# The output gate's panels of a gated linear attention, spread between its heads

## The chip, the cores and the metric

The kernel runs on one core of a Trainium2 chip. The metric is the device time of one execution in microseconds (us), as the median of several runs. TensorE is called PE, VectorE DVE, ScalarE ACT, SyncE SP, GpSimd POOL, as in the profile.

## The reference, cut to what matters

A decoder trunk of two layers over 256 tokens of width 2048, in fp32: a layer with gated linear attention (GLA), a layer with forgetting attention, cross-attention into 256 memory tokens in both, and a gated feed-forward network behind each. The change lies in the GLA layer alone, whose mixer is:

```python
def gla_mixer(h, mem_k, mem_v, w_in, w_gate_up, b_gate, gn_gain, w_out):
    z = h @ w_in
    q, k, v, glr, og, mq = split_cols(z, [...])
    g = jax.nn.log_sigmoid((glr @ w_gate_up + b_gate).astype(jnp.float32)) / GLA_GATE_TAU
    o = gla_chunked(split_heads(q, 4) * (256 ** -0.5), split_heads(k, 4), split_heads(v, 4), split_heads(g, 4))
    o = o * lax.rsqrt(jnp.mean(o * o, axis=-1, keepdims=True) + EPS)
    o = o * gn_gain.astype(jnp.float32).reshape(4, 1, 384)
    o = merge_heads(o).astype(h.dtype) * jax.nn.silu(og)
    m = memory_attention(mq, mem_k, mem_v)
    return jnp.concatenate([o, m], axis=-1) @ w_out
```

There are 4 heads with keys of 256 and values of 384. The output gate `og` has 1536 columns; it meets the heads' normed output only in the product with `silu(og)`.

## The kernel before

Every projection goes through weight panels. A panel's weights come from HBM in units of 512 KB (384 KB for values) on SP's queue (L198); each unit is split by ACT into a rounded part `whi` (a cast, L201) and by DVE into the residual `wlo` (L210). There are 4 buffers for raw units, 3 for `whi` and 4 for `wlo`. `proj_fm` multiplies a panel of 256 columns: 4 units, for each of two 128-column halves 16 matmuls with `whi` over 512 columns (L239) and 16 with `wlo` over 256 (L237). Its result has the features on the partitions; `whole` adds its two halves (ACT L246, DVE L248). `proj_tm` multiplies a panel of values or of the output projection, in 8 units (L276); a unit is 12 matmuls.

The GLA function takes the heads one after the other; they are called head 0 to head 3 here. For each head stand, in the program's order: the gates (`gates`: a matmul L585, then Abs, Exp and Ln on ACT at L588 to L590, and on DVE L592 to L594, which gives `bc`), the panels for q and k, the panel for v (head 0's v was made ahead), and the core (`core`). The core builds decays with Exp on ACT (L603, L604, L610, L626, L633) and products on DVE, runs small matmuls (L646 to L668), copies their results through masks into `att` (DVE L677, L690), multiplies by v (L697, L698, through the single buffer `ps_o`, which ACT empties at L701), and norms the result (L339, a Newton iteration of small DVE instructions, `dg` at L373, the matmuls L375, the row L378 and the scaling L706) into `on`, three 128-wide slices for each head.

`take_og(j)` multiplies panel j of the output gate, which covers the slices 2j and 2j+1, and makes the mix: DVE L713, Silu on ACT (L714), the product with `on` (DVE L715), and a split into two parts (ACT L311, DVE L312). Slices 0 to 2 need head 0, 3 to 5 head 1, 6 to 8 head 2, 9 to 11 head 3. The gate's tile takes one of five buffers with the tag `tmp`, which the gates of the heads use too. Before, panels 0 and 1 stand behind head 3's k and ahead of its v, and panels 2 to 5 behind head 3's core. The output projection follows; it takes the memory heads' slices 12 to 15 first, then 0 to 11 in order.

A planner sets the order of instructions on each engine from the program's order, priorities (weight units are drawn ahead by 300 instructions) and its own estimates. A core's first matmuls are held until the last projection panel of values has ended (`issue_after(ends[-1].ins)`). Each engine then works strictly in its order. Where the functions of ACT change between table sets, the builder puts in loads of the table.

Of the kernel before, what the change touches and what calls it, by code (L numbers as in the profile page):

```python
# [25 lines left out]
GLA_H, DK, DV = 4, 256, 384  # L26
# [11 lines left out]
NUNIT = 1024  # L38
AHEAD = 300

OG_EARLY = 2
WARM = 12

FV_PARTS = ((0, 376), (376, 764), (764, 1152), (1152, 1536))
# [10 lines left out]
def _panels():  # L55

    full = list(range(KC))
    out = []  # L60

    def fm(key, w, c0, kcs=full, second=None):
        cols = [(c0, 256)] if second is None else [(c0, 128), (second, 128)]
        out.append((key, w, kcs, cols, 4))

    def tm(key, w, c0, n, kcs=full, more=()):
        out.append((key, w, kcs, [(c0, n), *more], 2))

    for l in range(2):
        for j in range(2):  # L70
            fm(("mk", l, j), ("mem_w_kv", l), j * 256)
        tm(("mv", l), ("mem_w_kv", l), 512, 512)
    tm(("gv", 0), ("gla_w_in", 0), G_V, DV, more=[(G_R, RANK)])
    for j in range(2):
        fm(("mq", 0, j), ("gla_w_in", 0), G_MQ + j * 256)
    for h in range(GLA_H):
        fm(("gq", h), ("gla_w_in", 0), G_Q + h * DK)
        fm(("gk", h), ("gla_w_in", 0), G_K + h * DK)
        for j in range(OG_EARLY if h == GLA_H - 1 else 0):
            fm(("og", j), ("gla_w_in", 0), G_OG + j * 256)  # L80
        if h:
            tm(("gv", h), ("gla_w_in", 0), G_V + h * DV, DV)
    for j in range(OG_EARLY, 6):
        fm(("og", j), ("gla_w_in", 0), G_OG + j * 256)
    late = list(range(12, 16)) + list(range(12))

    def ffn(l):
        for p, (lo, hi) in enumerate(PARTS):
            for j in range(lo, hi):
                fm(("up", l, j), ("ffn_w_up", l), j * P, second=HID + j * P)  # L90
            for f in range(4):
                tm(("down", l, p, f), ("ffn_w_down", l), f * 512, 512, list(range(lo, hi)))

    for f in range(4):
        tm(("wo", 0, f), ("gla_w_out", 0), f * 512, 512, late)
    ffn(0)
    for j in range(6):
        fm(("fk", j), ("fox_w_kv", None), F_K + j * 256)
    for j, (lo, hi) in enumerate(FV_PARTS):
        more = [] if j else [(F_L, FOX_H)]  # L100
        tm(("fv", j), ("fox_w_kv", None), F_V + lo, hi - lo, more=more)
    for j in range(2):
        fm(("mq", 1, j), ("fox_w_in", 0), FOX_H * HD + j * 256)
    for j in range(6):
        fm(("fq", j), ("fox_w_in", 0), j * 256)
    for f in range(4):
        tm(("wo", 1, f), ("fox_w_out", 0), f * 512, 512, late)
    ffn(1)
    return out
# [29 lines left out]
def _trunk(ctx: ExitStack, tc: tile.TileContext, xt, xtok, memt, wp, wgu, gns, gfin, cnv, par, msk, out):  # L139
# [73 lines left out]
    def proj_fm(key, src, evac, before=None):  # L213

        units = where[key]
        acc = [pacc.tile([P, 512], F32, name="acc", tag="acc") for _ in range(2)]
        base = min(min(u[1]) for u in units)
        if before is None:  # L220
            turns = [(0, 0), (1, 0), (0, 1), (1, 1), (2, 1), (3, 1), (2, 0), (3, 0)]
        else:
            turns = [(0, 0), (0, 1), (1, 0), (1, 1), (2, 0), (2, 1), (3, 1), (3, 0)]
        ready = {}
        for u, low in turns:
            if u not in ready:
                if before is None:
                    ready[u] = split_unit(units[u])
                else:
                    ready[u] = split_unit(units[u], 2, lambda half: before(u, half), whole=u > 0)  # L230
            w = ready[u][low]
            for j, kc in enumerate(units[u][1]):
                both = src[kc - base]
                for c in range(2):
                    s = slice(j * 256 + c * P, j * 256 + (c + 1) * P)
                    if low:
                        TE.matmul(acc[c][:, :T], w[:, s], both[:, 0, :], start=False, stop=False)  # L237
                    else:
                        TE.matmul(acc[c], w[:, s], both, start=u == j == 0, stop=(u, j) == (3, 3))  # L239
        for c in range(2):  # L240
            evac(c, acc[c])

    def whole(a):

        t = sm.tile([P, T], F32, name="part1", tag="part1")
        S.activation(t, a[:, T:], AF.Copy)  # L246
        r = sm.tile([P, T], F32, name="wholes", tag="wholes")
        V.tensor_tensor(r, a[:, :T], t, ALU.add)  # L248
        return r
# [57 lines left out]
    def split(dst, i, src, g=None):  # L307

        hi, lo = dst[i][:, 0, :], dst[i][:, 1, :]
        if g is None:  # L310
            S.activation(hi, src, AF.Copy)  # L311
            V.tensor_tensor(lo, src, hi.bitcast(F32), ALU.subtract)  # L312
        else:
            S.activation(hi, src, AF.Copy, scale=g)
            V.scalar_tensor_tensor(lo, src, g, hi.bitcast(F32), ALU.mult, ALU.subtract)  # L315
# [93 lines left out]
    def place(buf, i, name, dtype=F32R):  # L409

        return const.tile([P, 2, T], dtype, name=f"{name}{i}", tag=f"{buf}{i}")
# [119 lines left out]
    def gla(nx):  # L531
        h, mix = bufB, bufA
        with tc.tile_pool(name="gla", bufs=1) as gp:
# [9 lines left out]
            def values(hd):  # L543
                return gp.tile([P, 2, DV], F32, name="gv", tag="gv", bufs=2)
# [29 lines left out]
            def gates(hd):  # L574

                bc = gp.tile([P, 2, T], F32, name="bc", tag="bc", bufs=2)
                raw = gp.tile([P, DK], F32, name="wgraw", tag="wgraw")
                nc.sync.dma_start(raw, wgu[hd])
                wg = gp.tile([P, DK], F32R, name="wg", tag="wg")
                S.activation(wg, raw, AF.Copy)  # L580
                V.tensor_tensor(wg[32:64], raw[32:64], wg[32:64].bitcast(F32), ALU.subtract)
                for c in range(2):
                    f = 2 * hd + c
                    ps = work("s", 2)
                    TE.matmul(ps[:, :T], wg[:, c * P : (c + 1) * P], glr, start=True, stop=True)  # L585
                    bias = part[:, C_BG + f : C_BG + f + 1]
                    e = gp.tile([P, T], F32, name="ge", tag="tmp", bufs=5)
                    S.activation(e, ps[:, :T], AF.Abs, bias=bias)  # L588
                    S.activation(e, e, AF.Exp, scale=-1.0)
                    S.activation(e, e, AF.Ln, bias=1.0)  # L590
                    mz = gp.tile([P, T], F32, name="gm", tag="tmp", bufs=5)
                    V.tensor_scalar(mz, ps[:, :T], bias, 0.0, ALU.add, ALU.min)  # L592
                    V.tensor_tensor(mz, mz, e, ALU.subtract)
                    V.tensor_tensor_scan(bc[:, c, :], scanmask, mz, 0.0, ALU.mult, ALU.add)  # L594
                return bc
# [112 lines left out]
            def take_og(j):  # L708
                def evac(c, a):
                    i = 2 * j + c  # L710
                    mix[i] = place("A", i, "mix")
                    g = gp.tile([P, T], F32, name="gate", tag="tmp", bufs=5)
                    V.tensor_tensor(g, whole(a), nx.row(), ALU.mult)  # L713
                    S.activation(g, g, AF.Silu)  # L714
                    V.tensor_tensor(g, g, on[i], ALU.mult)  # L715
                    split(mix, i, g)

                proj_fm(("og", j), h, evac)

            for hd in range(GLA_H):  # L720
                bc = gates(hd)
                q = gp.tile([P, 2, T], F32, name="gq", tag="gq", bufs=2)
                k = gp.tile([P, 2, T], F32, name="gk", tag="gk", bufs=2)
                v = values(hd) if hd else v0
                proj_fm(("gq", hd), h, lambda c, a: V.scalar_tensor_tensor(
                    q[:, c, :], whole(a), DK ** -0.5, nx.row(), ALU.mult, ALU.mult))
                proj_fm(("gk", hd), h, lambda c, a: V.tensor_tensor(k[:, c, :], whole(a), nx.row(), ALU.mult))
                if hd == GLA_H - 1:
                    for j in range(OG_EARLY):
                        take_og(j)  # L730
                if hd:
                    proj_tm(("gv", hd), h, lambda b, a: S.activation(
                        v[:, b, :], a, AF.Copy, scale=nx.col()[:, b : b + 1]))
                core(hd, q, k, v, bc)
            for j in range(OG_EARLY, 6):
                take_og(j)


# [146 lines left out]
    def preparing(name, dst, also=None):  # L885
# [18 lines left out]
        return n, then  # L904

    gla(nx)
    n, then = preparing("ffn0", bufB)
    add_out(("wo", 0), bufA, then)
# [132 lines left out]
```

## Time and profile before

| | us |
|---|---|
| median of 3 runs (2284.77 to 2284.79) | 2284.78 |
| the profiled execution | 2284.61 |
| its span | 2282.8 |
| PE busy | 2270.1 (99%) |
| DVE busy | 1602.8 (70%) |
| ACT busy | 1249.9 (55%) |

The heads of the GLA layer run between about 160 and 330 us of the span, the output projection from 379 us on. In a row of a timeline or of groups, `x` is the number of instructions, and `<-` names what released a wait.

### The profile page before, as it was taken

How to read it: one execution, taken by the hardware profiler on the slowest of the kernel's cores; microseconds unless marked ns; L12 is line 12 of the kernel's file. 1: busy time of each engine (PE TensorE's matmuls, PEld its weight loads, DVE VectorE, ACT ScalarE, POOL GpSimd, SP SyncE). 2: the span in 40 equal slices, each digit the busy share in tenths (PEclk: the TensorE clock that was granted, in tenths of full speed). 3: DMA queues.
4: the chain of work that ended last, by engine and by line, in shares of the span. 5: the costliest groups of instructions: out<-in, count | busy, mean ns of one | idle time of the engine just before them, and what ended most of it. 6: DMA issues, size and time to landing. Idle time of an engine off the chain costs nothing.

```text
span 2282.8 us, 33321 instructions
## 1 busy us (share of the span) xinstructions
PE 2270.1 (99%) x12420; PEld 1984.6 (87%) x12420; DVE 1602.8 (70%) x2691; ACT 1249.9 (55%) x1981; POOL 3.4 (0%) x19
## 2 busy tenths in 40 slices
PE   9999999999999999999999999999999999999998
PEld 8989988888888888888888998888888888888886
DVE  8579987577765777557766567657776577756775
ACT  7565555555643555445565556556554455534554
POOL 0000000000000000000000000000000000000000
PEclk9999999999999999999999999999999999999999
DMA  9655556555666565666655665555656556665664
GB/s 327 197 165 160 161 160 192 187 184 185 185 200 193 186 195 185 194 191 188 194 185 184 180 198 160 174 190 184 193 186 194 187 192 191 192 194 186 190 193 155
DMA packets 125034, 430.16 MB, mean 188 GB/s; under 512 B 14140, under 2 KB 19144, under 8 KB 124744
## 3 DMA queue, kind: packets, MB, share of 16 engines
q1 hardware_dynamic: 124440, 427.24, 59.3%
q8 instruction: 97, 1.59, 0.3%
q10 hardware_dynamic: 432, 0.79, 0.1%
q14 instruction: 65, 0.53, 0.1%
HBM read 425.87 MB, written 2.11 MB: 187 GB/s over the span
## 4 chain that ended last, share of the span: by engine, by line
PE 98%; DVE 2%; issue 0%; DMA 0%; ACT 0%; DVEq 0%
PE acc L239 38%; PE acc L276 36%; PE acc L237 20%; DVE wlo L210 1%; PE ps_s L898 0%; PE ps_t L407 0%; PE ps_s L653 0%; PE ps_o L428 0%; PE ps_s L428 0%; DVE A L315 0%; PE ps_s L810 0%; PE ps_o L826 0%; DVE att L690 0%; PE ps_o L697 0%; DMA raw<-wp 0%
## 5 line engine op out<-in xcount | busy, mean ns | idle before, releaser
L210 DVE TENSOR_TENSOR wlo<-raw,whi 128x1024 fp32r<-128x1024 f32 (+4 forms) x812 | 970.9, 1197 | 581.2 <-ACT whi L201 578.4
L201 ACT ACTIVATE whi<-raw 128x1024 fp32r<-128x1024 f32 (+4 forms) x812 | 841.1, 1037 | 746.0 <-PE acc L276 341.1
L239 PE MATMUL acc<-B,whi 128*128 128x512 f32 x2112 | 503.4, 391 | 0.0
L239 PEld LDWEIGHTS acc<-B,whi 128*128 128x128 f32 x2112 | 389.0, 188 | 75.9
L276 PE MATMUL acc<-whi,mix 128*128 128x512 f32 x1280 | 320.2, 390 | 0.0
L239 PE MATMUL acc<-mix,whi 128*128 128x512 f32 x1248 | 307.7, 391 | 0.0
L276 PEld LDWEIGHTS acc<-whi,mix 128*128 128x128 f32 x1280 | 239.7, 188 | 49.8
L237 PEld LDWEIGHTS acc<-B,wlo 128*128 128x128 f32 x2112 | 267.8, 191 | 9.5 <-DVE wlo L210 1.8
L237 PE MATMUL acc<-B,wlo 128*128 128x256 f32 x2112 | 273.3, 283 | 1.4 <-DVE wlo L210 1.4
L239 PEld LDWEIGHTS acc<-mix,whi 128*128 128x128 f32 x1248 | 228.9, 188 | 44.1
L276 PE MATMUL acc<-whi,B 128*128 128x512 f32 (+3 forms) x960 | 217.6, 362 | 0.0
L276 PEld LDWEIGHTS acc<-whi,B 128*128 128x128 f32 x960 | 174.7, 188 | 17.9
L276 PE MATMUL acc<-wlo,mix 128*128 128x512 f32 x640 | 174.8, 390 | 0.0
L237 PE MATMUL acc<-mix,wlo 128*128 128x256 f32 x1248 | 163.1, 284 | 0.0
L237 PEld LDWEIGHTS acc<-mix,wlo 128*128 128x128 f32 x1248 | 158.3, 191 | 4.5
L276 PEld LDWEIGHTS acc<-wlo,mix 128*128 128x128 f32 x640 | 119.8, 188 | 24.5
L239 PE MATMUL acc<-A,whi 128*128 128x512 f32 x544 | 134.7, 391 | 0.0
L246 ACT ACTIVATE part<-acc 128x256 f32<-128x256 f32 x240 | 90.9, 379 | 61.6 <-PE acc L239 61.2
L276 PE MATMUL acc<-wlo,B 128*128 128x512 f32 (+3 forms) x480 | 121.4, 363 | 0.0
L239 PEld LDWEIGHTS acc<-A,whi 128*128 128x128 f32 x544 | 101.8, 189 | 21.1 <-DVE A L315 0.2
L872 ACT ACTIVATE cv<-u,cw 128x256 f32<-128x256 f32 x176 | 105.0, 598 | 24.6 <-DVE u L868 24.6
L248 DVE TENSOR_TENSOR wholes<-acc,part 128x256 f32<-128x256 f32 x240 | 100.2, 418 | 0.5 <-ACT part L246 0.2
(224 smaller groups left out, 1605.8 us busy)
## 6 DMA issues: line engine op xcount, KB each, us to landing
raw<-wp SPq DMA_DIRECT2D x743, 512.0 KB, 3.7
raw<-wp SPq DMA_DIRECT2D x32, 384.0 KB, 3.5
raw<-wp SPq DMA_DIRECT2D x24, 388.0 KB, 3.5
raw<-wp SPq DMA_DIRECT2D x8, 400.0 KB, 3.1
xf<-xt SPq DMA_DIRECT2D x16, 128.0 KB, 4.5
x<-xtok SPq DMA_DIRECT2D x4, 512.0 KB, 6.4
mt<-memt SPq DMA_DIRECT2D x3, 512.0 KB, 6.3
cb<-cdram SPq DMA_DIRECT2D x12, 128.0 KB, 3.1
```

The lines of the kernel that those rows point to most:

```text
L201: casts.append(S.activation(hi[:, s], raw[:, s], AF.Copy))
L210: V.tensor_tensor(lo[:, s], raw[:, s], hi[:, s].bitcast(F32), ALU.subtract)
L237: TE.matmul(acc[c][:, :T], w[:, s], both[:, 0, :], start=False, stop=False)
L239: TE.matmul(acc[c], w[:, s], both, start=u == j == 0, stop=(u, j) == (3, 3))
L246: S.activation(t, a[:, T:], AF.Copy)
L248: V.tensor_tensor(r, a[:, :T], t, ALU.add)
L276: mm = TE.matmul(acc[b][:, :n], src[kc - base][:, part, xs], w, start=u == 0 and low == part == j == 0, stop=u == end and low == 1 and j = ...
L872: S.activation(r, u[:, 2:], AF.Identity, bias=w[3], scale=w[2])
```

## The change

One panel of the output gate moves ahead of head 1's values, one ahead of head 2's, two (panels 2 and 3) stand ahead of head 3's, and panels 4 and 5 behind its core. The list of panels in HBM and the program's order change together. Nothing is computed differently.

```diff
-OG_EARLY = 2
+OG_AT = {1: (0,), 2: (1,), 3: (2, 3)}
...
         fm(("gk", h), ("gla_w_in", 0), G_K + h * DK)
-        for j in range(OG_EARLY if h == GLA_H - 1 else 0):
+        for j in OG_AT.get(h, ()):
             fm(("og", j), ("gla_w_in", 0), G_OG + j * 256)
         if h:
             tm(("gv", h), ("gla_w_in", 0), G_V + h * DV, DV)
-    for j in range(OG_EARLY, 6):
+    for j in range(4, 6):
         fm(("og", j), ("gla_w_in", 0), G_OG + j * 256)
...
                 proj_fm(("gk", hd), h, lambda c, a: V.tensor_tensor(k[:, c, :], whole(a), nx.row(), ALU.mult))
-                if hd == GLA_H - 1:
-                    for j in range(OG_EARLY):
-                        take_og(j)
+                for j in OG_AT.get(hd, ()):
+                    take_og(j)
                 if hd:
                     proj_tm(("gv", hd), h, lambda b, a: S.activation(
                         v[:, b, :], a, AF.Copy, scale=nx.col()[:, b : b + 1]))
                 core(hd, q, k, v, bc)
-            for j in range(OG_EARLY, 6):
+            for j in range(4, 6):
                 take_og(j)
```

## The prediction

> **What bounds the kernel now.** I read the page's busy shares first, then TensorE's waits, then a table of windows over the gated-linear-attention (GLA) part, then the timelines around the two waits.
>
> ```profile
> span 2282.8 us, 33321 instructions
> ...
> PE 2270.1 (99%) x12420; PEld 1984.6 (87%) x12420; DVE 1602.8 (70%) x2691; ACT 1249.9 (55%) x1981; POOL 3.4 (0%) x19
> ```
>
> ```profile
> PE acc L237 <- DVE wlo L210: 1.6, 2, 1.4
> PE ps_o L697 <- DVE att L690: 1.1, 1, 1.1
> ```
>
> TensorE (PE) works 2270.1 of 2282.8 us, so moving panels can save only idle time; the waits above are each us in all, times, longest. Two places carry them (start, length, instructions, idle before in brackets):
>
> ```profile
> 279.02 0.67 PE L697 MATMUL ps_o<-att,gv 128*128 128x256 f32 x2 [1.11 <-DVE att L690]
> ...
> 294.19 1.22 PE L237 MATMUL acc<-B,wlo 128*128 128x256 f32 x8 [1.38 <-DVE wlo L210]
> ...
> 313.57 1.55 PE L276 MATMUL acc<-whi,B 128*128 128x384 f32 x8
> ...
> 315.65 1.55 PE L276 MATMUL acc<-whi,B 128*128 128x384 f32 x8
> ...
> 345.16 0.60 PE L697 MATMUL ps_o<-att,gv 128*128 128x256 f32 x2
> ...
> 360.33 4.00 PE L237 MATMUL acc<-B,wlo 128*128 128x256 f32 x32
> 364.16 5.64 PE L239 MATMUL acc<-B,whi 128*128 128x512 f32 x24
> 369.64 0.28 PE L375 MATMUL ps_t<-dg,onesr 128*128 128x256 f32 x1
> ```
>
> Both come from VectorE (DVE), 1.11 + 1.38 = 2.49 us, while head 3's q, k and the first output-gate (og) panels run. The last rows give PE's rates: 32 matmuls of 256 columns in 3.83 us (0.12 each), 24 of 512 in 5.48 (0.228), a 384-wide unit of 12 in 2.08. An og panel (32 + 32 matmuls) is therefore 11.1 us of PE, wherever it stands. Why DVE is late is in the windows (us, then PE, weight loads, DVE and ACT busy): the whole head stretch, the tail behind it, and the three windows from one head's mask copies (L677) to the next head's.
>
> ```profile
> 160.00:320.00 160.00, 157.45 (x1084) 144.23 (x1083) 151.74 (x375) 97.57 (x176) 0.00 (x0) 1.00 0.50 155
> 320.00:380.00 60.00, 60.00 (x404) 54.16 (x404) 43.52 (x95) 31.46 (x53) 0.00 (x0) 1.00 0.59 180
> 194.57:231.72 37.15, 37.15 (x273) 34.78 (x272) 35.55 (x85) 23.19 (x41) 0.00 (x0) 1.00 0.56 176
> 231.72:270.68 38.96, 38.96 (x287) 36.69 (x287) 37.76 (x102) 22.78 (x42) 0.00 (x0) 1.00 0.50 157
> 270.68:332.51 61.83, 59.28 (x395) 54.08 (x395) 54.93 (x136) 36.95 (x65) 0.00 (x0) 1.00 0.53 166
> ```
>
> DVE is busy 151.7 of 160 us among the heads, 43.5 of 60 behind them, with ACT at 97.6 and the granted clock 1.00. PE bounds the kernel; DVE is all but level with it here. All numbers are for this profiled execution: 2284.61 us, 1.8 over its span; the three runs' median is 2284.78, 0.17 more, which I add at the end. A measurement of this kernel can tell about 0.2%, 4.6 us, from no change.
>
> **The change part by part.** I compared the changed kernel's order of instructions on each engine with this one's. PE's is the same up to head 1's values and again from early in the output projection's second panel; matmuls are as many as before. Weight loads move with their panels on SyncE's queue; nothing is added there, and where the loads of the gate weights (L578) now stand, the buffers they wait for come free before those of the weight units behind them: nothing.
>
> *Moved DVE work.* An og panel brings DVE four residual casts (L210), and for two slices each an addition, two products and a residual (L248, L713, L715, L312).
>
> ```profile
> L210 DVE TENSOR_TENSOR wlo<-raw,whi 128x1024 fp32r<-128x1024 f32 x63 | 76.6, 1220 | 20.3 <-ACT whi L201 19.8
> L210 DVE TENSOR_TENSOR wlo<-raw,whi 128x768 fp32r<-128x768 f32 x24 | 22.8, 953 | 2.9 <-ACT whi L201 2.7
> L248 DVE TENSOR_TENSOR wholes<-acc,part 128x256 f32<-128x256 f32 x29 | 12.1, 419 | 0.4 <-ACT part L246 0.2
> ```
>
> With 0.42 for each 256-wide piece that is 4 x 1.22 + 8 x 0.42 = 8.2 us beside PE's 11.1: each panel gives DVE up to 2.9 us of air. Head 3's window had two panels and keeps two. The window from head 1's mask copies to head 2's gains PE 11.1 us (38.96 to 50.1) and DVE more than one panel's work, since og 0's products with head 0's normed output fall into it too: 5 casts, 4 additions and 9 pieces of gates, 5 x 1.22 + 13 x 0.42 = 11.6 (37.76 to 49.3). It stays level: no air where it was wanted.
>
> *Added table loads.* The diff does not show this. Silu (L714) belongs to another set of ACT's tables than the heads' Exp and Ln. Before, all Silus come behind the last head's Exps, and one load serves (first row). In the changed order ACT's queue goes Exp, Silu, Ln, Silu, Exp among heads 1 to 3, and once Silu has been in, the builder loads separately for Exp and for Ln: I count 21 loads in place of 7, 15 in place of one in GLA. An Exp–Ln pair of that kind runs later in this kernel (second fence):
>
> ```profile
> 305.05 1.28 ACT L714 ACT_TABLE_LOAD   x1
> 308.50 0.82 ACT L714 ACTIVATE gate<-gate 128x256 f32<-128x256 f32 x2 [2.16 <-DVE gate L713]
> ```
>
> ```profile
> 1291.69 0.48 ACT L760 ACTIVATE fe<-ps_s,part 128x256 f32<-128x256 f32 x1 [0.32 <-PE ps_s L302]
> 1292.18 1.28 ACT L761 ACT_TABLE_LOAD   x1
> 1293.48 0.42 ACT L761 ACTIVATE fe<-fe 128x256 f32<-128x256 f32 x1
> 1293.80 0.84 ACT L201 ACTIVATE whi<-raw 128x776 fp32r<-128x776 f32 x1
> ```
>
> Abs ends at 1292.17, Exp begins at 1293.48: 1.30 us, or 1.4 for independent neighbours, which otherwise overlap by 0.1 (Exp's 0.42 from 1293.48 reaches past the cast's start at 1293.80). Fourteen are 18.2 us more for ACT, on 97.6 in 160: it has the room in sum, but it works in order, and behind a load stand the casts (L201) that PE and DVE want and the evacuations (L701) that free the single ps_o. [...]
>
> ACT's pieces:
>
> ```profile
> L201 ACT ACTIVATE whi<-raw 128x1024 fp32r<-128x1024 f32 x63 | 66.6, 1058 | 44.2 <-PE acc L239 18.4 <-PE acc L276 7.1 <-issue 5.4
> L201 ACT ACTIVATE whi<-raw 128x768 fp32r<-128x768 f32 x24 | 20.3, 846 | 21.2 <-PE acc L239 12.3 <-PE acc L276 7.0 <-DVE att L690 1.2
> ...
> L714 ACT ACTIVATE gate<-gate 128x256 f32<-128x256 f32 x12 | 4.9, 413 | 2.2 <-DVE gate L713 2.2
> L701 ACT ACTIVATE onorm<-ps_o 128x256 f32<-128x256 f32 x12 | 4.6, 380 | 6.5 <-PE ps_o L698 6.5
> ```
>
> Now each window, from the end of a head's last L668:
>
> - *A, head 0's core beside og 0 and head 1's values.* PE runs 24 x 0.228 + 32 x 0.12 + 0.24 + 2 x 0.6 + 5 x 2.08 = 21.2 us to the sixth unit of values. ACT starts on head 0's first output (L701) when PE has done 21 x 0.228, 32 x 0.12, one L585 and the first pair of L697 and L698 (0.6): 9.4, with the hand-over 9.5. Up to that unit's cast lie 4 casts (0.85), a 384-wide Exp and 14 smaller pieces (0.4), 9.5 us less 0.1 each for overlap = 7.6, and 4 loads at 1.4 = 5.6: ready at 22.7. PE waits 1.5; the bounds are 0 (ACT has the casts done ahead of the loads) and 5.6 (all four show). I take 1.5, the sum. DVE, which waits on the same queue, comes into the next window some 1.5 late.
> - *B, head 1's core beside head 2's q and k and og 1.* DVE is level with PE (49.3 to 50.1), comes 1.5 late and waits for one load (1.3) in the middle of its gate chain. og 1's casts stand in the first half, before the window's 0.8 of margin has come: late by 1.5 + 1.3 = 2.8, which I take; at least 1.5 - 0.8 = 0.7 (the load hides), at most 1.5 + 3 x 1.3 = 5.4 (three loads stand in that chain).
> - *C, head 2's core beside head 3's q and k.* 4 loads stand between the first gate matmul (L585, behind 16 x 0.228 + 27 x 0.12 = 6.9) and the evacuation that frees ps_o for the head's third L697, due at 19.5 (head 3's q, 11.1; two pairs of L697 and L698 and two L585, 1.4; in k another 16 and 27, 6.9). ACT: 4 casts at 1.06, 11 pieces at 0.4, less 1.4 overlap = 7.2, plus 5.6, from 7.3: 20.1, with the hand-overs about 20.5. PE waits 1.0 (0 to 3). Behind that two og panels and values give DVE 4 us and more: no other wait.
> - *Tail: two panels behind head 3 in place of four.* PE reaches the output projection 22.2 us earlier, but head 3's norm does not come earlier:
>
> ```profile
> 365.55 0.76 DVE L373 TENSOR_TENSOR dg<-mask,y 128x256 fp32r<-128x256 f32 x2
> ...
> 372.56 1.27 DVE L706 SCALAR_TENSOR_TENSOR onorm<-onorm,part,row 128x256 f32<-128x256 f32 x3
> ```
>
> The dg stands 33 us behind the mask copies of 332.51. The projection starts 24 behind them (two panels, 22.2, and three pairs of L697 and L698) and goes through 6 units (12 x 0.228 = 2.7) before it needs slice 8, at 40.4, and slice 9 after 12 matmuls more (2.7), at 43.1: the order puts the next panel's first 8 there. L375 stands in the sixth unit (38.6), so row and three onorms are done at 41 and slice 9 at 42. Cover 1 us; expected cost 0, up to 3 if the row slips.
>
> Sum: -2.49 + 1.5 + 2.8 + 1.0 + 0 = +2.8: 2284.61 + 2.8 + 0.17 = **2287.6 us**, +0.12%, within what counts as no change; by the upper bounds 5.6 + 5.4 + 3 + 3 - 2.5 = +14.5, by the lower -2.49 + 0.7 = -1.8. [...]
>
> **The rivals.**
> 1. *Slower: DVE pays for the loads.* Eight loads stand between a piece that DVE hands to ACT and the one it waits for back (gate halves and the first Exp on bc, heads 1 to 3). DVE has 8.3 us idle in 160, so if ACT is never ahead, all land on PE: 8 x 1.3 = 10.4 for 2.49, +7.9: 2284.61 + 7.9 + 0.17 = 2292.7. For: DVE's queue is in order and full. Against: the loads run ahead of their operands (305.05, while Silu came at 308.50 when DVE delivered), so part hides. It decides from over 7.1 us of PE waits in A to C. 0.27.
> 2. *The loads hide and the old waits go*: each panel's 2.9 us of air covers both, 2284.61 - 2.49 + 0.17 = 2282.3. For: ACT is idle 62 of 160 us. Against: window B gets no air. 0.15.
> [...]
> 4. *Faster by over 0.2%*: PE would need 4.6 us; it idles 2.49 here. 0.01.
>
> **How the numbers follow.** Forecast (2284.0 to 2289.4) 0.54, rivals 0.27, 0.15, 0.03, 0.01. Within 0.2%: 0.54 + 0.15 = 0.69; slower 0.27 + 0.03 = 0.30; faster 0.01. The range takes in rival 2 and most of rival 1: 2282.0 to 2292.5.
>
> **What would show it.** 15 table loads of 1.28 in GLA; no wait of 1.11 and 1.38 as above, but waits of PE on a values cast (L276 <- L201) beside head 1's values, on L210 in og 1, on L701 beside head 3's k; none in the tail. Wrong if PE idles over 7 us among the heads, if the loads show gaps behind them, or if the output projection waits for mix.

## The result, and the profile after

The changed kernel takes 2288.64 us (median of 22 runs, 2287.23 to 2289.83); the kernel before, 2284.78 (22 runs, 2284.55 to 2285.03). That is +3.86 us, a ratio of 1.0016 with a 95% interval of 1.0010 to 1.0022: within what was counted as no change, on the slow side. The profiled execution took 2288.87 us, with a span of 2287.1.

Busy time of the engines, then TensorE's waits over the whole span (us in all, times, longest):

```profile
PE 2273.3 (99%) x12420; PEld 1986.0 (87%) x12420; DVE 1604.8 (70%) x2691; ACT 1266.4 (55%) x1995; POOL 3.4 (0%) x19
```

```profile
PE acc L237 <- DVE wlo L210: 2.9, 3, 1.8
...
PE ps_o L697 <- ACT onorm L701: 0.5, 1, 0.5
PE acc L276 <- ACT whi L201: 0.3, 1, 0.3
```

ACT does 16.5 us more with 14 instructions more: the table loads, of 1.28 us each. The two old waits are gone (no L697 waits for att any more), and others stand in their place. PE's busy time grew by 3.2 us although it executes the same 12420 matmuls: some of them run slower. The timeline of PE shows where (idle before in brackets):

```profile
217.17 1.68 PE L276 MATMUL acc<-whi,B 128*128 128x384 f32 x8 [0.32 <-ACT whi L201]
...
258.39 1.22 PE L237 MATMUL acc<-B,wlo 128*128 128x256 f32 x8 [0.62 <-DVE wlo L210]
261.44 1.47 PE L237 MATMUL acc<-B,wlo 128*128 128x256 f32 x8 [1.83 <-DVE wlo L210]
262.71 2.76 PE L276 MATMUL acc<-whi,B 128*128 128x384 f32 x8
...
310.52 0.70 PE L697 MATMUL ps_o<-att,gv 128*128 128x256 f32 x2 [0.45 <-ACT onorm L701]
...
383.46 1.99 PE L276 MATMUL acc<-whi,A 128*128 128x512 f32 x8
```

The eight matmuls at 262.71 take 2.76 us; eight of that shape took 1.55 in the kernel before. The windows around them (us; PE, weight loads, DVE, ACT busy; the third number from the end is the granted clock):

```profile
258.79:262.20 3.41, 1.58 (x13) 1.38 (x13) 3.41 (x10) 3.10 (x4) 0.00 (x0) 1.00 0.37 115
262.20:265.61 3.41, 3.41 (x14) 3.41 (x14) 3.32 (x7) 0.53 (x2) 0.00 (x0) 0.50 0.49 137
```

In 3.41 us PE worked 1.58; for the 3.41 us behind that its clock was granted at half. The last row of the timeline is the output projection's first: 383.46, against 379.23 before. All of the loss therefore arises ahead of it (0.36 of these 4.23 us already at the start of the kernel, where two short waits fell differently), and behind it neither kernel's PE waits.

### The profile page after: what moved, and what is told of

Same layout as the page of the kernel before. It is cut to its first block, busy times and chain, and to the rows that moved or that the text cites. A ratio compares the mean times of both kernels' runs of the same rounds, so it can differ in the third digit from the quotient of the medians.

```text
span 2287.1 us, 33330 instructions
## 1 busy us (share of the span) xinstructions
PE 2273.3 (99%) x12420; PEld 1986.0 (87%) x12420; DVE 1604.8 (70%) x2691; ACT 1266.4 (55%) x1995; POOL 3.4 (0%) x19
## 4 chain that ended last, share of the span: by engine, by line
PE 97%; ACT 1%; DVE 1%; issue 0%; DMA 0%; SPq 0%; DVEq 0%
PE acc L239 38%; PE acc L276 36%; PE acc L237 20%; PE ps_s L897 0%; PE ps_s L653 0%; DVE wlo L210 0%; PE ps_t L407 0%; ACT whi L201 0%; PE ps_o L428 0%; PE ps_s L428 0%; DMA mt<-memt 0%; PE ps_s L809 0%; PE ps_o L825 0%; PE ps_o L697 0%; PE ps_s L808 0%
## 5 line engine op out<-in xcount | busy, mean ns | idle before, releaser
L210 DVE TENSOR_TENSOR wlo<-raw,whi 128x1024 fp32r<-128x1024 f32 (+4 forms) x812 | 970.9, 1197 | 576.6 <-ACT whi L201 574.2
```

The costliest lines, as they stand in the source:

```text
L210: V.tensor_tensor(lo[:, s], raw[:, s], hi[:, s].bitcast(F32), ALU.subtract)
```

## The experiments

Theory 1 was the prediction's: the table loads hold up ScalarE's queue, and the new waits come from that. Theory 2: the places of the panels cost by themselves, and the loads hide. "Before" is the kernel before, run beside each; its median was 2284.66 to 2284.75.

**The loads taken out, all else kept.** PE's and DVE's orders of instructions are the changed kernel's, one for one.

```
-                    S.activation(g, g, AF.Silu)
+                    S.activation(g, g, AF.Silu if j > 3 else AF.Copy)
```

> The changed kernel with Silu left out of og panels 0 to 3 (Copy in its place, so their gates are not the reference's; panels 4 and 5 keep it): TensorE's and VectorE's orders are those of the changed kernel instruction for instruction, and only the 14 extra table loads are gone. Theory 1 (the loads make ScalarE late, and TensorE's waits in heads 1 to 3 and the half-clock stretch behind them come from that): those waits go and with them the 3.4 us at half clock, so the time falls to 2282.0 to 2283.5, below the kernel before, since the two old waits of 1.11 and 1.38 us are not there either. Theory 2 (where the panels stand is what costs: VectorE is level with TensorE beside head 2's q and k, and the loads hide in ScalarE's idle time): the time stays at 2287 to 2289.

Measured: 2286.29 us (11 runs, 2284.95 to 2287.5), ratio to before 1.0007 (0.9998 to 1.0016). Neither theory: 2.35 us below the changed kernel, yet 1.6 above the kernel before. The three windows from one head's last L668 to the next one's, first of the changed kernel, then of this one, say where the loads cost:

```profile
194.55:233.37 38.82, 38.50 (x283) 35.70 (x279) 35.09 (x83) 27.74 (x47) 0.00 (x0) 1.00 0.50 159
233.37:290.21 56.84, 54.27 (x358) 49.43 (x354) 51.84 (x134) 37.56 (x62) 0.00 (x0) 0.97 0.52 162
290.21:358.49 68.28, 67.83 (x452) 62.10 (x448) 57.86 (x131) 46.37 (x73) 0.00 (x0) 1.00 0.53 167
```

```profile
194.21:232.04 37.83, 37.83 (x283) 35.79 (x279) 36.01 (x90) 23.03 (x43) 0.00 (x0) 1.00 0.53 172
232.04:288.32 56.28, 53.99 (x358) 49.49 (x355) 50.72 (x128) 30.95 (x57) 0.00 (x0) 0.97 0.49 159
288.32:355.87 67.55, 67.55 (x453) 62.02 (x449) 58.32 (x131) 38.95 (x67) 0.00 (x0) 1.00 0.52 168
```

The loads cost 0.99 in the first, 0.56 in the second and 0.73 in the third, 2.28 together, close to the 2.35 between the medians. In the middle window PE idles 2.3 us without any load, and the clock is 0.97 there as well. PE and, at the same place, VectorE:

```profile
256.51 1.22 PE L237 MATMUL acc<-B,wlo 128*128 128x256 f32 x8 [0.46 <-DVE wlo L210]
259.57 1.73 PE L237 MATMUL acc<-B,wlo 128*128 128x256 f32 x8 [1.84 <-DVE wlo L210]
261.10 2.62 PE L276 MATMUL acc<-whi,B 128*128 128x384 f32 x8
```

```profile
253.70 1.62 DVE L625 TENSOR_TENSOR gdd<-bc 128x256 f32<-128x256 f32 x5
255.24 1.22 DVE L210 TENSOR_TENSOR wlo<-raw,whi 128x1024 fp32r<-128x1024 f32 x1
256.38 1.21 DVE L625 TENSOR_TENSOR gdd<-bc 128x384 f32<-128x384 f32 x3
257.48 0.56 DVE L605 TENSOR_TENSOR gq<-gq,ge 128x384 f32<-128x384 f32 x1
257.95 0.43 DVE L248 TENSOR_TENSOR wholes<-acc,part 128x256 f32<-128x256 f32 x1
258.29 1.23 DVE L210 TENSOR_TENSOR wlo<-raw,whi 128x1024 fp32r<-128x1024 f32 x1
```

No row of VectorE has an idle time: it works without a break, and between the cast that ends the first wait (255.24) and the one that ends the second (258.29) stand five pieces of head 2's gates and k. This wait is VectorE's queue, not ScalarE's loads.

**The loads alone.** Orders of PE and DVE are the kernel before's; behind one Silu on a gate weight the builder loads separately for Exp and for Ln, 12 more loads.

```
-                S.activation(wg, raw, AF.Copy)
+                S.activation(wg, raw, AF.Silu if hd == 2 else AF.Copy)
```

> The kernel before with one Copy of a gate weight (for head 2) replaced by Silu, so that gate is not the reference's; from there on Exp and Ln load a table each, as in the changed kernel: 12 more loads among heads 1 to 3, and TensorE's and VectorE's orders are untouched. Theory 1 (loads): the two old waits stay and the loads' waits come on top; without the air of a moved panel at least the changed kernel's time, 2288 to 2293. Theory 2 (placement): loads alone cost nothing, 2284.5 to 2285.5.

Measured: 2289.98 us (9 runs, 2289.37 to 2291.17), ratio 1.0024 (1.0015 to 1.0034): +5.3. As theory 1 had it. PE's waits in the heads:

```profile
PE acc L237 <- DVE wlo L210: 3.2, 3, 1.4
PE ps_o L697 <- DVE att L690: 1.2, 1, 1.2
PE acc L276 <- DVE wlo L210: 1.0, 1, 1.0
PE acc L239 <- ACT whi L201: 0.8, 1, 0.8
```

The old two (1.2 and 1.4) stand, with 3.6 us of new ones. Without a moved panel, 12 loads cost 5.3 us; with the panels, 14 cost 2.35. That fits panels that give the air which the prediction spoke of and loads that use it up, though the loads do not stand at the same places in the two kernels.

**Fewer loads.** The set with both Exp and Ln is loaded again behind each Silu of og 0 and 1.

```
+                    if j < 2:
+                        with tc.issue_after(silu.ins):
+                            S.preload_act_table_set("natural_log_exp_and_others")
```

> The changed kernel, with the table set that holds both Exp and Ln loaded again right behind each Silu of og panels 0 and 1: two loads for each of these four Silus, but none any more between Exp and Ln of heads 2 and 3; 10 loads in the heads in place of 15. Theory 1 (loads, by where they stand): the waits beside head 2's q and k and head 3's k shrink, the one beside head 1's values stays at about 1; 2283 to 2286.5. Theory 2 (placement): 2287 to 2289.

Measured: 2289.03 us (9 runs, 2288.99 to 2291.49), ratio 1.0022 (1.0013 to 1.0032). Theory 1's number was missed: a third of the loads gone (none stands between 216.5 and 278.2 us, where the changed kernel has four between 243.2 and 254.7) and nothing won. ScalarE's timeline beside head 1's values, and PE's there:

```profile
211.07 1.28 ACT L717 ACT_TABLE_LOAD   x1
212.37 0.39 ACT L701 ACTIVATE onorm<-ps_o 128x256 f32<-128x256 f32 x1
212.65 0.84 ACT L201 ACTIVATE whi<-raw 128x768 fp32r<-128x768 f32 x1
213.50 1.28 ACT L714 ACT_TABLE_LOAD   x1
...
215.23 1.28 ACT L717 ACT_TABLE_LOAD   x1
```

```profile
216.86 0.96 PE L276 MATMUL acc<-wlo,B 128*128 128x384 f32 x4 [1.06 <-DVE wlo L210]
218.24 2.23 PE L276 MATMUL acc<-whi,B 128*128 128x384 f32 x8 [0.42 <-ACT whi L201]
```

Five loads now stand between 207.6 and 216.5, where the changed kernel has four; PE waits 1.5 there in place of 0.3, and the eight matmuls at 218.24 run at a lowered clock (0.50 from 219.10 on, rows in the last section). The profiled run (2290.04) is one of four with a mean clock of 0.998; the median is one of five at 2288.99 to 2289.03 with 0.999, to be set beside the changed kernel's six at 2287.23 to 2287.52 with 0.999. All three engines also work in another order here than in the changed kernel. So the rows suggest that it counts how many loads stand in one stretch, and not only how many there are, but this run does not show it by itself.

**The last part alone.**

```
+OG_AT = {3: (0, 1, 2, 3)}
```

> Only the last part of the change: og panels 0 to 3 all ahead of head 3's values, two behind, none among heads 1 and 2. One table load for Silu, as before. My term for the tail was 0, with up to 3 if head 3's norm comes late for the output projection. Both theories: the two old waits of 1.11 and 1.38 us stay (they lie ahead of the moved panels), no wait at the output projection: 2284.3 to 2285.3. If two panels are too little cover: a wait at the output projection's slice 8 or 9, up to 2288.

Measured: 2285.03 us (11 runs), ratio 1.0002 (0.9993 to 1.0011). Both old waits are there (1.14 and 1.38) and PE waits for nothing at the output projection: two panels cover head 3's norm. The 0.37 us above before have no wait to their name. The profiled run is 0.51 above before's; at the last matmul only 0.14 of it is there, 0.13 from the first 17 us of the kernel, and the rest lies behind the last matmul, away from the change.

**Silu later.** Raw gates of og 0 and 1 are parked in their slots of buffer A, and Silu, product and split come behind head 3's core.

```
+                    if j < 2:
+                        late[i] = place("A", i, "late", F32)[:, 0, :]
+                        V.tensor_tensor(late[i], whole(a), nx.row(), ALU.mult)
+                        return
```

> The changed kernel with all panels where they are, but the raw gates of og 0 and og 1 parked in their slots of buffer A, and their Silu, product and split done behind head 3's core: one table load for Silu, as in the kernel before, and 1.6 us of gate work less on VectorE ahead of og 1's residual casts. Theory 1 (loads make the waits beside head 1's values and head 3's k, VectorE's queue ahead of og 1's casts makes the ones in og 1): the first two go; of the 2.3 us in og 1, 1.6 go, and with less than a microsecond of idle the clock stays whole: 2282.3 to 2283.5. Theory 2 (og 1's weight units come late by themselves, whatever VectorE has ahead of them): the wait and the half clock stay, 2285.5 to 2287. Rival for the end: the moved gate work makes the output projection wait for its slices 0 to 3, up to 3 us more.

Measured: 2283.36 us (11 runs, seven at 2283.25 to 2283.59, four at 2284.82 to 2284.90), ratio 0.9996 (0.9988 to 1.0005). The time is as expected, the step to it only half: the waits in og 1 are 0.59 and 1.05, 0.66 less, not 1.6. The order is the scheduler's, and it put other work into the gap: eight subtractions of head 2's gates, where five stood before the first of these casts, so that it starts at 255.38, no earlier than in the kernel with Copy (255.24):

```profile
252.26 2.73 DVE L625 TENSOR_TENSOR gdd<-bc 128x256 f32<-128x256 f32 x8
254.91 0.55 DVE L605 TENSOR_TENSOR gq<-gq,ge 128x384 f32<-128x384 f32 x1
255.38 1.22 DVE L210 TENSOR_TENSOR wlo<-raw,whi 128x1024 fp32r<-128x1024 f32 x1
```

The larger part of the 2.9 us below the kernel with Copy comes from two other places: the trace has no half clock (mean 0.999), and head 1's two L375 no longer stand among head 2's L653 (below), which takes 2.03 us in place of 3.11. What sets the four runs at 2284.8 to 2284.9 apart, no trace shows.

**Where the early panel stands, with Silu late.** og 0 ahead of head 1's values, og 1 to 3 ahead of head 3's:

```
+OG_AT = {1: (0,), 3: (1, 2, 3)}
```

> As late_silu, but only og 0 stands early (ahead of head 1's values); og 1 to 3 all stand ahead of head 3's values. No panel beside head 2. Theory 1: VectorE has the heads' work of the kernel before from head 2 on, so the two old waits of 1.11 and 1.38 us come back, lessened by what og 0's panel left VectorE ahead: 2283.0 to 2284.8, no half clock. Theory 2: any early panel costs by itself: over 2285.

Measured: 2282.61 us (11 runs), ratio 0.9991 (0.9982 to 1.0). Below the range of either theory: the old waits do not come back; one of 1.1 us is left beside head 2's values. With og 0 ahead of head 2's values instead:

```
+OG_AT = {2: (0,), 3: (1, 2, 3)}
```

> As late_silu, but only one panel stands early, og 0 ahead of head 2's values, and og 1 to 3 ahead of head 3's. Theory 1: head 1's stretch is the kernel before's; og 0's casts beside head 2's k come with less gate work ahead of them than og 1's had, a wait of 0 to 1, and behind the panel the two old waits are gone: 2282.3 to 2283.8. Theory 2: the wait of 2.3 us in the panel beside head 2 and the half clock come with any panel put there: 2285 to 2287.

Measured: 2283.57 us (11 runs), ratio 0.9996 (0.9987 to 1.0005), waits of 0.16 and 0.56 behind it, beside head 2's values, and no half clock (mean 0.999): a panel beside head 2 need not cost 2.3 us. And both og 0 and og 1 ahead of head 1's values, og 2 and 3 ahead of head 3's:

```
+OG_AT = {1: (0, 1), 3: (2, 3)}
```

> As the version with only og 0 ahead of head 1's values and its Silu done late (2282.61), but og 0 and og 1 both stand there, og 2 and 3 ahead of head 3's values. TensorE gets 11.1 us more beside head 0's core. If what is gained there on VectorE carries over to head 2's stretch, the wait of 1.1 us beside head 2's values shrinks: 2281.3 to 2282.4. If VectorE can only be ahead by the few buffers of residual weights, it stays: 2282.4 to 2283.0. If a panel fewer beside head 3 brings back the old waits there: 2283 to 2285.

Measured: 2282.00 us (11 runs, 2281.5 to 2282.18), ratio 0.9987 (0.9979 to 0.9996): 2.75 us below before and 6.6 below the changed kernel, the best version. What VectorE gains beside head 0's core does carry over. PE's waits in the heads, all of them, and the busy times:

```profile
PE ps_t L375 <- DVE dg L373: 0.4, 1, 0.4
```

```profile
PE 2268.5 (100%) x12420; PEld 1983.5 (87%) x12420; DVE 1604.1 (70%) x2691; ACT 1249.8 (55%) x1981; POOL 3.4 (0%) x19
```

**The half clock.** Six matmuls against a zero tile fill PE's idle time in og 1; first with the loads (the changed kernel), then without them (the first experiment's kernel).

```
+            if key == ("og", 1) and (u, low) in ((1, 1), (2, 1)):
+                for i in range(2 * u):
+                    TE.matmul(acc[i % 2], zero, src[0], start=False, stop=False)
```

> The changed kernel with six matmuls of 512 columns against a zero tile (0.23 us each; they add zero) put into og 1 on TensorE, two ahead of its second and four ahead of its third wlo group, where TensorE waited 0.6 and 1.8 us. Table loads and VectorE's work are as in the changed kernel. Theory 1 (TensorE's clock falls to half for 3.4 us because it stood idle for most of the stretch before): the waits are filled, the clock stays at 1.00, and the time falls by the 1.3 us by which the changed kernel's own runs differ, to 2287.2 to 2287.6, although TensorE has 1.4 us more to do. Theory 2 (the slow matmuls there have another cause, such as late weights): no fall, 2288.4 to 2290.

Measured: 2290.55 us (9 runs, 2290.32 to 2292.03), ratio 1.0026 (1.0016 to 1.0036), above the range of either theory. The granted clock stays at 1.00, and the fourth wlo group of og 1 starts at 264.21 in place of 265.80, 1.6 us earlier; but then PE waits beside head 3's q and k, where the changed kernel has one wait of 0.45 (line numbers are 6 higher here):

```profile
303.98 2.10 PE L245 MATMUL acc<-B,whi 128*128 128x512 f32 x8 [0.25 <-ACT whi L204]
308.09 0.70 PE L703 MATMUL ps_o<-att,gv 128*128 128x256 f32 x2 [0.83 <-ACT onorm L707]
310.56 1.21 PE L243 MATMUL acc<-B,wlo 128*128 128x256 f32 x8 [0.84 <-DVE wlo L213]
312.48 2.12 PE L245 MATMUL acc<-B,whi 128*128 128x512 f32 x8 [0.71 <-ACT whi L204]
```

The gain is lost again in the next stretch with four loads. The order of the matmuls there differs too, so how much of that is the loads' own stays open.

> The same six matmuls against a zero tile in og 1, on the kernel without the extra table loads (Copy in place of Silu in og panels 0 to 3, so their gates are not the reference's), where TensorE waits 0.46 and 1.84 us in og 1 and runs at half clock behind it. Theory 1 (idle time makes the half clock, worth 1.3 us): the clock stays at 1.00 and all runs come out as the two quickest of that kernel did, 2284.8 to 2285.3, in place of its median of 2286.29. Theory 2 (the slow matmuls have another cause): 2286.2 or more.

Measured: 2285.19 us (11 runs, 2285.08 to 2285.49), ratio to before 1.0002 (0.9993 to 1.0011): 1.1 us below the same kernel without the fill, and all runs within 0.4. Theory 1. The same stretch without the fill and with it:

```profile
256.60:260.05 3.45, 1.61 (x12) 1.41 (x13) 3.45 (x8) 3.41 (x5) 0.00 (x0) 0.99 0.33 114
260.05:263.46 3.41, 3.41 (x15) 3.41 (x14) 3.41 (x8) 0.53 (x1) 0.00 (x0) 0.51 0.45 120
```

```profile
256.60:260.05 3.45, 2.54 (x14) 1.82 (x14) 3.45 (x8) 3.45 (x6) 0.00 (x0) 1.00 0.39 114
```

The order of matmuls differs here too, but only behind og 1, and the gain is there before that: og 1's fourth wlo group starts at 262.80 in place of 263.92. So six matmuls that compute nothing make this kernel 1.1 us faster; in the changed kernel, with its loads, the same six made it 1.9 slower.

## Why the prediction came out as it did

The time was forecast at 2287.6 and is 2288.64, within 0.2% as forecast. What the prediction named as signs is all there: 15 loads of 1.28 us, the old waits gone, a wait on a values cast beside head 1's values (217.17), on L210 in og 1 (258.39, 261.44), on L701 beside head 3's k (310.52), none in the tail. The sizes are another matter. The loads were put at 5.3 us in the sum (1.5, 2.8 and 1.0) and cost 2.35. Three costs were in no term: VectorE's own queue in og 1, the half clock, and the place of two L375. These errors nearly cancel, so that the time came out within 1.1 us is in good part luck.

- **Old waits gone, -2.49: right.** Neither the changed kernel nor the one without loads has them.
- **A, +1.5: right in mechanism and place, 0.99 in size.** The sixth unit's cast was ready 22.6 us into the window (217.17 less 194.55), forecast 22.7; but PE came there at 22.3, not at 21.2. The step that failed is PE's own sum: it had two pairs of L697 and L698 on that way, and three stand there, 0.6 more; the other 0.5 are spread over the matmuls. Of the 0.99, half is lost at that wait and half over the next two units: PE starts the sixth unit at 217.17 and the eighth at 222.31, in the kernel with Copy at 216.35 and 220.97, and 0.34 of that difference stood before.
- **B, +2.8: by luck near the waits that are there (0.62 + 1.83), which have another reason.** It was made up of loads alone, 1.5 passed on from A and 1.3 for a load in VectorE's gate chain. The window with loads is only 0.56 longer than without; so much later VectorE comes to the first of og 1's two late casts (257.12, below, 23.75 us into the window; 255.24 without loads, 23.20 into it). Without any load the waits are 0.46 + 1.84. The failed step is "level with PE": it gave VectorE's own queue no term, and a sum over 50 us says nothing about the 3 us ahead of the cast that is waited for.

```profile
257.12 1.22 DVE L210 TENSOR_TENSOR wlo<-raw,whi 128x1024 fp32r<-128x1024 f32 x1
```

- **C, +1.0: right in mechanism and place, 0.73 in size.** PE came to the third L697 at 19.9 us into the window and could start at 20.3 (310.52 less 290.21); forecast were 19.5 and 20.5.
- **Tail, 0: right**, shown with the last part alone.
- **The half clock was in no term.** Its price is 1.1 us by the kernel with Copy, with and without the fill, and 1.3 by the changed kernel's own runs, which fall into two groups: 15 of 22 at 2288.38 to 2288.87 with a mean clock of 0.998, six at 2287.23 to 2287.52 with 0.999.
- **The norm's matmuls were in no term.** Head 1's two L375 now stand among head 2's L653, where those of the kernel before had PE's full-width matmuls around them:

```profile
286.31 0.88 PE L653 MATMUL ps_s<-gdd,gk 128*64 128x96 f32 x16
...
287.60 0.38 PE L375 MATMUL ps_t<-dg,onesr 128*128 128x256 f32 x1
...
289.41 0.40 PE L662 MATMUL ps_s<-gq,gk 128*64 128x64 f32 x8
```

From the first L653 to L662 that is 3.10 us; head 2's took 2.03 in the kernel before:

```profile
266.14 0.88 PE L653 MATMUL ps_s<-gdd,gk 128*64 128x96 f32 x16
...
268.17 0.40 PE L662 MATMUL ps_s<-gq,gk 128*64 128x64 f32 x8
```

The two L375 are 0.24 of the difference by themselves, so their place costs 0.8. The traces of all twelve kernels agree: this group takes 2.03 or 2.04 us in every head with no L375 inside, 2.61 with one (the kernel with fewer loads), and 3.10 to 3.12 with two.

So without loads, waits of 2.3, a half clock of 1.2 and 0.8 for L375, less 2.5, make +1.8 (measured +1.6); the loads add 2.35; together about the +3.9. Rival 1 (VectorE pays for the loads) needed over 7.1 us of PE waits in A to C, and they are 3.2; but where no panel stands, 12 loads cost 5.3, and most of the new waits there are on VectorE. Rival 2 (loads hide, old waits go, 2282.3) fails: the old waits do go, but the loads cost 2.35, and without them the time is still 2286.29. Only the versions with Silu late come near its number, 2283.36 with the panels as given and 2282.00 with both in head 1, and they move VectorE's work too. The chance of 0.03 in the forecast was for a stop of ScalarE behind each load, as long again as the load; no run shows one: in the kernel with fewer loads the load at 211.07 ends at 212.35 and the next instruction starts at 212.37, so the load took 1.28 us and the gap behind it 0.02; behind 14 of the changed kernel's 15 loads in GLA the gap is 0.01 or 0.02.

## What to carry to other kernels

Moving work so that it covers a wait can carry along an activation function from another table set; count the table loads in the built program's order, and put the foreign function where no other set is needed behind it (here, for og 0 and 1, the time went from 2288.64 to 2283.36 us, though not by the loads alone). When an engine is level with the bottleneck over a window, walk its queue in front of each piece that the bottleneck waits for, since the window's sum hides a wait of 2 us. And look at the granted clock behind a wait of the matmul engine, since the wait can cost more than its length: here 1.8 us of waiting, behind which the clock was granted at 0.50 for 3.41 us, cost 1.1 to 1.3 us more.

## What was not expected of the hardware

TensorE's clock fell to half with no long pause ahead of it. One wait of 1.83 us left PE busy for 1.58 of the 3.41 us up to 262.20, and the next 3.41 us ran at half clock (0.50); the wait of 0.62 had ended at 258.39, ahead of that stretch. In the kernel before, the wait of 1.38 left it 1.96 busy in the 3.40 us up to 294.40, and the clock stayed whole (1.00); so it did with the fill, at 2.54 of 3.45. Where the boundary lies stays open: in the kernel with fewer loads, two stretches with 1.93 us of work each went different ways.

```profile
215.69:219.10 3.41, 1.93 (x10) 1.51 (x10) 2.98 (x5) 3.40 (x7) 0.00 (x0) 1.00 0.38 111
219.10:222.51 3.41, 3.41 (x12) 3.41 (x11) 3.17 (x10) 3.41 (x7) 0.00 (x0) 0.50 0.60 204
260.06:263.47 3.41, 1.93 (x12) 1.53 (x12) 3.41 (x8) 3.41 (x6) 0.00 (x0) 1.00 0.31 115
263.47:266.88 3.41, 3.01 (x21) 3.01 (x22) 3.41 (x9) 1.04 (x2) 0.00 (x0) 1.00 0.37 118
```

The changes of the clock lie on a grid in the traces of the changed kernel and of the kernel before. In the changed kernel's the first record of the granted clock, at full, is at 6.21 us, and it falls to half at 262.21, 75 times 3.4133 us later; the half lasts 3.413 us. It falls again at 2282.90, behind the last matmul, 591 times 3.4133 after the end of that half. In the kernel before, the first record is at 7.56 and the only fall at 2277.42, also behind the last matmul, 665 times 3.4133 later. What sets the grid, no run shows. Among the heads the drops came with no gap over 1.84 us.
